# Casting two weight blocks ahead of the bank copies, and making the last block's sum sooner, in the seven-product groups of three feed-forwards

## The chip, the cores and the metric

The kernel runs on one core of a Trainium2 chip, as one program. The metric is the time of one execution on the device in microseconds; the median of several runs counts. Beside the runs there is one profiled execution, from which all rows below are taken.

## The reference, cut to what matters

A two-layer encoder trunk over 256 tokens of width 1024, all in float32. Each layer is a feed-forward, a token mixer (a convolution in the first layer, latent attention in the second), and another feed-forward. So there are four feed-forwards, and all four have the same shape:

```python
D_MODEL = 1024; SEQ = 256; D_FF = 2816

def swiglu_ffn(h, w1, w3, w2):
    return (jax.nn.silu(h @ w1) * (h @ w3)) @ w2

for i in range(DEPTH):
    h = h + FFN_RES_WEIGHT * swiglu_ffn(rmsnorm(h, ffn_norm1[i]), ffn1_w1[i], ffn1_w3[i], ffn1_w2[i])
    m = rmsnorm(h, mix_norm[i])
    ...  # h = h + conv_module(m, ...) or mla(m, ...)
    h = h + FFN_RES_WEIGHT * swiglu_ffn(rmsnorm(h, ffn_norm2[i]), ffn2_w1[i], ffn2_w3[i], ffn2_w2[i])
return rmsnorm(h, final_norm)
```

## The kernel before, in words

**Split numbers.** Each float32 operand is split into a high part (`hi`, rounded to the matmul's type) and a low part (`lo`, what the rounding left). A product of two operands is then three matmuls: low weights by high rows, high by high, high by low rows (`mm3`, lines 333, 336, 337). ScalarE casts the high part of a weight block (`hi<-raw`), VectorE subtracts it for the low part (`lo<-raw,hi`); each block is split in two pieces of 1024 columns, so there are two casts and two subtractions for each.

**Blocks.** Weights come as blocks of 128 x 2048 from memory, by SP's queue, into four `raw` buffers; `hi` and `lo` have five buffers each (`W_BUFS`). The list `blocks` holds them in the order of use. `load_to(n)` loads and splits blocks up to number n; `n_used` counts those in use.

**Seven products for eight.** In the up products of a feed-forward there are six chunks (c = 0 to 5) of 512 columns of `w1` and of `w3`. For chunk 3 (`SEVEN_UP`), and for the first part of the down products, the kernel replaces eight block products by seven, on sums and differences of blocks and of rows (`seven_products`). Such a group uses seven split blocks, here called block one to seven; in the code they are `n0` to `n0 + 6`, and `load_seven` makes them with j = 0 to 6. Blocks five and six are split from `raw` buffers that earlier subtractions left (j = 4 and 5). Block seven is split from one that has to be made first by a subtraction over the whole block, 128 x 2048 (`sub(b[11], b[21], b[11])`, called the sum of block seven). Block eight is the first block of chunk 4.

**The group's order.** Each of the seven products is 12 matmuls (four slices of rows, three each) into one of four accumulator banks, `c11`, `c21`, `c12`, `c22` in the code, `u` in the profile. Product one goes to c11; ScalarE then copies c11 to c21. Product two goes to c22; ScalarE copies c22 to SBUF (`kept`, in the profile `p`). Product three accumulates into c21; VectorE adds c21 and kept into c12 (the first addition of banks). Product four accumulates into c11, product five into c21, and VectorE adds c21 and kept into c22 (the second addition). Product six accumulates into c12, product seven into c21. So product five, which writes c21, has to wait for the first addition, which reads it. After the group ScalarE takes the activation of the first rows of tokens from c11 and of the second from c21, VectorE multiplies, and the result is turned (`gt` transpose, four transfers `gd`, one transfer `gb`) into the gates `Gh` and `Gl` for the down products.

**What sets the order.** The program is recorded in the order of the code and then scheduled once, at build time, by priorities and dependencies; each engine afterwards works through its own list in order. `urgent(...)` records an instruction with high priority, `order(a, b)` makes a come after b on the list. The lines that matter here: casts of a block are kept `behind` the last urgent instructions, and one low piece of block six and one of block seven come after the first and the second addition (`order(casts[n0 + 5, 0][1], add.ins)` and the same with 6).

Of the kernel before, what the change touches and what calls it, by code (L numbers as in the profile page):

```python
# [15 lines left out]
AF = mybir.ActivationFunctionType  # L16
# [26 lines left out]
PIECES = 2  # L43
# [46 lines left out]
def trunk(ctx: ExitStack, tc: tile.TileContext, x, xt, first, pos, invf, gfin, wdw,  # L90
          f1w13, f1w2, f2w13, f2w2, cw1, cw2, wa, wuq, wukv, wo, wpair, out):
    nc = tc.nc
# [12 lines left out]
    def uid(s):  # L105
        n_uid[0] += 1
        return f"{s}_{n_uid[0]}"
# [6 lines left out]

    def seven(four):

        group = {}
        return [("seven", j, four, group) for j in range(7)]  # L120

    blocks = []
    conv_block = {}
    for i in range(2):
        for w13, w2 in ((f1w13, f1w2), (f2w13, f2w2)):

            n_ffn = 2 * i + (w13 is f2w13)
            for cc_ in range(5):
                if cc_ in SEVEN_UP.get(n_ffn, ()):
                    four = [w13[i, m, 2 * cc_ + a_] for a_ in range(2) for m in range(2)]  # L130
                    blocks += seven(four)
                    continue
                for m in range(2):
                    blocks += [w13[i, m, 2 * cc_ + a_] for a_ in range(2)]
            blocks += [w13[i, a_, 10] for a_ in range(2)]
            if n_ffn in SEVEN_DOWN:
                blocks += seven([w2[i, a_] for a_ in range(4)])
            blocks += [w2[i, a_] for a_ in range(4 if n_ffn in SEVEN_DOWN else 0, NF // 2)]
            if w13 is f1w13:
                if i == 0:  # L140

                    for m in (-1, -2, -3, -4, *CONV_TILES):
                        blocks += [cw2[-m - 1] if m < 0 else ("whole", cw1[m])]
                        conv_block[m] = len(blocks) - 1
                else:
                    blocks += [wa[0], wa[1], wa[2][:, :1280], wa[3][:, :1280]]
                    blocks += [wuq[2], wuq[0], wukv[0], wukv[1], wuq[1]]
                    blocks += [wo[a_] for a_ in range(H // 2)]
    loaded = []
    n_used = [0]  # L150
# [3 lines left out]
    def order(ins, first):  # L154
        tc.add_manual_dep(ins.ins, first.name, mybir.DependencyInfo(
            mybir.DependencyClass.NoSync, mybir.DependencyReason.DATA), reason="order")

    def behind(ins):

        for first in ahead_of.get(ins.ins.engine, [])[-BEHIND:]:  # L160
            order(ins, first)


    casts = {}
# [18 lines left out]
    def fetched(src):  # L183
        raw = rawp.tile([P, HB], F32, tag="raw", name=uid("raw"))
        dma = nc.sync.dma_start(raw, src)
        if turns:
            order(dma, turns[-1].ins)
        return raw

    def load_seven(j, four, b, pieces):  # L190
        hi = wp.tile([P, HB], F32R, tag="hi", name=uid("hi"))
        lo = wp.tile([P, HB], F32R, tag="lo", name=uid("lo"))
        n = len(loaded)
        if j == 0:
            b[11], b[12] = fetched(four[0]), fetched(four[1])
        elif j == 1:
            b[22] = fetched(four[3])
        elif j == 2:
            b[21] = fetched(four[2])
        def sub(out, left, right):  # L200
            ins = nc.vector.tensor_sub(out, left, right)  # L201
            behind(ins)
            return ins

        if j == 1:
            sub(b[11], b[12], b[11])
            sub(b[12], b[22], b[12])
        elif j == 2:
            thirds[n] = sub(b[11], b[22], b[11])
        elif j == 6:  # L210
            sub(b[11], b[21], b[11])
        raw = b[(11, 11, 11, 21, 12, 22, 11)[j]]
        for i in range(pieces):
            c = slice(i * HB // pieces, (i + 1) * HB // pieces)
            casts[n, i] = nc.scalar.copy(hi[:, c], raw[:, c]), sub(lo[:, c], raw[:, c], hi[:, c].bitcast(F32))  # L215
            behind(casts[n, i][0])
        return hi, lo
# [35 lines left out]
    def urgent(f):  # L253

        def g(*args, **kw):
            traced = nc.cur_bb.bb.instructions
            n = len(traced)
            with tc.high_priority():
                r = f(*args, **kw)
            last = {ins.engine: ins for ins in traced[n:]}  # L260
            for engine, ins in last.items():
                ahead_of.setdefault(engine, []).append(ins)
            return r
        return g

    def load_ahead(ahead=W_BUFS - 2):
        load_to(min(len(blocks), n_used[0] + ahead))

    def load_to(last):
        while len(loaded) < last:  # L270
            loaded.append(load(blocks[len(loaded)], PIECES))
# [98 lines left out]
            out[n] = [z[:, i].rearrange("p (k t) -> p k t", t=P) for z in (sh, sl)]  # L370
        return out

    def seven_products(xh, xl, forms, banks, late={}):


        def rows(a, tb):
            k = slice(4 * a, 4 * a + 4)
            return xh[:, k, tbs(tb)], xl[:, k, tbs(tb)]

        def product(a, b, fresh):  # L380
            load_ahead(W_BUFS - 1)
            (hi, lo), = weights(1, False)
            for k in range(4):
                c = slice(k * 512, k * 512 + 512)
                before[:] = [mm3(b, a[0][:, k], a[1][:, k], hi[:, c], lo[:, c], fresh and k == 0, k == 3, before, True)]

        n0 = n_used[0]
        before = []
        c11, c21, c12, c22 = banks[0, 0], banks[1, 0], banks[0, 1], banks[1, 1]
        product(rows(0, 0), c11, True)  # L390
        first = urgent(nc.scalar.copy)(c21, c11)
        for cast in late.values():
            order(cast, first.ins)
        product(forms[0], c22, True)
        kept = tmp.tile([P, 512], F32, tag="s", name=uid("p5"))
        urgent(nc.scalar.copy)(kept, c22)
        product(forms[1], c21, False)
        add = urgent(nc.vector.tensor_add)(c12, c21, kept)
        order(casts[n0 + 5, 0][1], add.ins)
        for high, low in gates[-2 * NT:-NT] if not late else ():  # L400
            order(low, thirds[n0 + 2].ins)
        late_gates = []
        for high, low in gates[-NT:] if not late else ():
            late_gates.append((high, low))
        product(rows(1, 0), c11, False)
        product(forms[2], c21, False)
        add = urgent(nc.vector.tensor_add)(c22, c21, kept)
        order(casts[n0 + 6, 0][1], add.ins)
        for n, (high, low) in enumerate(late_gates):
            order(high, casts[n0 + 5 + n, PIECES - 1][0].ins)  # L410
            order(low, casts[n0 + 7, PIECES - 1][1].ins)
        product(forms[3], c12, False)
        product(rows(1, 1), c21, False)
# [8 lines left out]
    def tbs(tb):  # L422
        return slice(tb * P, (tb + 1) * P)
# [427 lines left out]
    def ffn_in(act, X, make_next, beside, apart, seven_up, seven_down):  # L851
# [48 lines left out]
        for c in range(6):  # L900

            both = c == 5
            w = 256 if both else 512
            kn = HB // 512
            u = {}
            if c == 0 and X.pool:
                first_chunk(X, u)
            if seven_up and c == min(seven_up) - 2:
                after = [casts[5, PIECES - 1][1]] if X.whole else ()
                forms = forms_of(sums_of_rows(*whole_rows(X.xh, X.xl, after)), Gh[:, 14:], Gl[:, 14:])  # L910
            if both and seven_down:
                down()
            if c in seven_up:
                for key in ((0, 0), (0, 1), (1, 1), (1, 0)):
                    u[key] = bank("A", "u")
                seven_products(X.xh, X.xl, forms, {(tb, m): b for (m, tb), b in u.items()})
                beside()
                beside()
            for m in range(0 if u else 1 if both else 2):
# [18 lines left out]
                for i, (k, tb, *kinds) in enumerate(steps):  # L938
                    hi, lo = parts[k // kn]
                    j = k % kn  # L940
# [26 lines left out]
                    beside()  # L967
            for tb in range(NT):
                s = tmp.tile([P, 512], F32, tag="s", name=uid("s"))
                nc.scalar.activation(s[:, :w], u[0, tb][:, :w], AF.Silu, scale=X.r[tb])  # L970
                mul = urgent(nc.vector.tensor_mul) if c in seven_up or c + 1 in seven_up else nc.vector.tensor_mul
                mul(s[:, :w], s[:, :w], u[0, tb][:, w:] if both else u[1, tb])
                turn(c, tb, w, s)
        o = Rows(Gh, Gl, NF, make_next is Final, seven_down)
        if seven_down:
            both = (xp.tile([P, KT, S], F32R, tag=tag, name=uid("rows")) for tag in ("Xh", "Xl"))
            late = {2: None, 3: None}
# [753 lines left out]
    class Rows512:  # L1731

        n = {"ht": 0, "hb": 0}
# [11 lines left out]
    def beside():  # L1745

        next(todo, None)

    X = Norm("ffn1_0", half=True)
    first_rows(X)  # L1750
    X.whole = True
    X = ffn(X, lambda act: Plain("mix_0", act), beside)
    for _ in todo:
        pass
    X = conv(X, lambda act: Norm("ffn2_0", half=True, turn_by_dma=rows))
    apart.close()
    X = ffn(X, lambda act: Norm("ffn1_1", half=True, turn_by_dma=rows), apart=True)
    X = ffn(X, lambda act: Norm("mix_1", turn_by_dma=rows), apart=True)
    cc, sn, _ = tables
    X = mla(X, lambda act: Norm("ffn2_1", half=True, turn_by_dma=rows), cc, sn)  # L1760
# [102 lines left out]
```

## Time and profile before

| | us |
|---|---|
| median of 3 runs | 892.23 |
| the runs | 892.22, 894.73, 892.23 |
| profiled execution | 891.44 |
| its span in the profile | 889.5 |
| TensorE busy | 882.0 (99%) |
| VectorE busy | 770.4 (87%) |
| ScalarE busy | 580.2 (65%) |
| TensorE's waits, in all | 1.4 |

The span is what lies between the first and the last instruction in the trace; 1.94 us of the profiled execution lie around it. In the rows PE is TensorE, DVE VectorE, ACT ScalarE, POOL GpSimd and SP the queue that issues transfers. L201 is line 201 of the kernel. A row of a timeline has the start in us from the span's start, the duration in us, the engine, line, operation and operands (written tile, then those read), and in brackets the idle time before it and what ended it. The three groups that the change touches are those of feed-forward two (its first matmul at 337.41 us), three (511.5 us) and four (774.4 us). Busy time of TensorE counts modelled ends of matmuls, so its short waits are better read from the starts of neighbouring matmuls.

### The profile page before, as it was taken

The numbers are of one execution on the slowest core, as the hardware profiler recorded it, in microseconds if no ns is written. First come the engines' busy times: TensorE is split into PE (matmuls) and PEld (weight loads), VectorE is DVE, ScalarE is ACT, GpSimd is POOL, SyncE is SP. The second block draws the span as 40 slices with busy tenths as digits, with TensorE's granted clock in tenths as the row PEclk, the third lists the DMA queues.
The fourth block names the chain that finished last, engine by engine and source line by source line (L and its number), as shares of the span: only waits on it lengthen the run. The fifth ranks groups of instructions, "written<-read, shape, count | busy, mean of one in ns | idle before, by whom it ended". The sixth has DMA issues, their size and how long they took to land.

```text
span 889.5 us, 12294 instructions
## 1 busy us (share of the span) xinstructions
PE 882.0 (99%) x4209; PEld 741.9 (83%) x4209; DVE 770.4 (87%) x1114; ACT 580.2 (65%) x1005; POOL 104.8 (12%) x227
## 2 busy tenths in 40 slices
PE   9999999999999999999999999999999999999997
PEld 7888887898988888888888888888899888888886
DVE  6899999789999998999498989995778689989973
ACT  7667868789887655657275465673676666474752
POOL 1000000079952000000010000001400010000000
PEclk9999999999999999999999999999999999999999
DMA  9884929834216855939759378495643549287541
GB/s 338 297 308 161 398 80 374 300 132 153 96 60 225 307 213 194 365 93 393 251 179 344 97 249 318 142 386 183 221 147 142 190 155 368 80 300 276 192 190 48
DMA packets 71054, 198.94 MB, mean 224 GB/s; under 512 B 12368, under 2 KB 41936, under 8 KB 51664
## 3 DMA queue, kind: packets, MB, share of 16 engines
q1 hardware_dynamic: 70560, 197.47, 61.9%
q8 instruction: 33, 0.54, 0.2%
q10 hardware_dynamic: 432, 0.69, 0.2%
q14 instruction: 29, 0.24, 0.1%
HBM read 181.87 MB, written 16.25 MB: 223 GB/s over the span
## 4 chain that ended last, share of the span: by engine, by line
PE 98%; DVE 1%; issue 0%; ACT 0%; ACTq 0%; DVEq 0%
PE u L333 17%; PE u L337 17%; PE u L336 17%; PE o L333 9%; PE o L337 9%; PE o L336 9%; PE u L1019 3%; PE gate L1019 3%; PE o L1255 3%; PE u L418 2%; PE sc L1616 1%; PE tp L453 1%; PE pairs L1062 1%; DVE lo L201 1%; PE a L337 1%; PE a L336 1%
## 5 line engine op out<-in xcount | busy, mean ns | idle before, releaser
L248 DVE TENSOR_TENSOR lo<-raw,hi 128x1024 fp32r<-128x1024 f32 (+1 forms) x228 | 266.8, 1210 | 29.2 <-ACT hi L247 28.5
L247 ACT CAST hi<-raw 128x1024 fp32r<-128x1024 f32 (+1 forms) x230 | 228.5, 1044 | 72.1 <-DMA raw<-in_f2w 24.3
L337 PE MATMUL u<-hi,Xl 128*128 128x512 f32 x592 | 230.4, 389 | 0.0
L336 PE MATMUL u<-hi,Xh 128*128 128x512 f32 x592 | 230.3, 389 | 0.0
L333 PE MATMUL u<-lo,Xh 128*128 128x512 f32 x592 | 230.2, 389 | 0.0
L215 ACT CAST hi<-raw 128x1024 fp32r<-128x1024 f32 x112 | 111.7, 1049 | 56.7 <-DVE raw L201 46.4
L201 DVE TENSOR_TENSOR lo<-raw,hi 128x1024 fp32r<-128x1024 f32 x112 | 132.0, 1215 | 6.6 <-ACT hi L215 6.5
L337 PEld LDWEIGHTS u<-hi,Xl 128*128 128x128 f32 x592 | 111.1, 188 | 23.6 <-DVE Xl L472 0.5
L336 PEld LDWEIGHTS u<-hi,Xh 128*128 128x128 f32 x592 | 111.1, 188 | 23.1
L333 PEld LDWEIGHTS u<-lo,Xh 128*128 128x128 f32 x592 | 111.1, 188 | 22.9
L333 PE MATMUL o<-lo,Gh 128*128 128x512 f32 (+1 forms) x276 | 106.7, 386 | 0.0
L336 PE MATMUL o<-hi,Gh 128*128 128x512 f32 (+1 forms) x276 | 106.5, 386 | 0.0
L337 PE MATMUL o<-hi,Gl 128*128 128x512 f32 (+1 forms) x276 | 106.5, 386 | 0.0
L444 POOL TENSOR_TENSOR ms<-ss 128x1 f32<-128x1 f32 x16 | 8.1, 509 | 592.8 <-ACT junk L436 592.8
L201 DVE TENSOR_TENSOR raw<-raw,raw 128x2048 f32<-128x2048 f32 x32 | 73.1, 2285 | 0.8 <-DMA raw<-in_f1w 0.2
L333 PEld LDWEIGHTS o<-lo,Gh 128*128 128x128 f32 x276 | 51.8, 188 | 10.6 <-DVE lo L201 0.2
L337 PEld LDWEIGHTS o<-hi,Gl 128*128 128x128 f32 x276 | 51.8, 188 | 10.5
L336 PEld LDWEIGHTS o<-hi,Gh 128*128 128x128 f32 x276 | 51.8, 188 | 10.4
L1108 DVE SCALAR_TENSOR_TENSOR acc<-V,dw,acc 128x128 f32<-128x128 f32 (+1 forms) x174 | 53.9, 390 | 0.0
L970 ACT ACTIVATE s<-u,R 128x512 f32<-128x512 f32 (+1 forms) x48 | 30.9, 647 | 29.5 <-PE u L337 28.7
L1129 ACT ACTIVATE prod<-V,dw 128x128 f32<-128x128 f32 (+1 forms) x128 | 45.6, 415 | 1.9 <-POOL Y L1130 1.0
L806 DVE SCALAR_TENSOR_TENSOR h<-o,rh,h 128x512 f32<-128x512 f32 (+1 forms) x18 | 12.9, 719 | 29.0 <-PE o L337 29.0
(269 smaller groups left out, 1306.6 us busy)
## 6 DMA issues: line engine op xcount, KB each, us to landing
raw<-in_f2w SPq DMA_DIRECT2D x66, 1024.0 KB, 5.6
raw<-in_f1w SPq DMA_DIRECT2D x62, 1024.0 KB, 6.9
raw<-in_cw SPq DMA_DIRECT2D x12, 1024.0 KB, 5.2
gd<-gt SPq DMA_DIRECT2D x160, 64.0 KB, 2.9
gb<-gd SPq DMA_DIRECT2D x24, 256.0 KB, 2.8
rows<-gd SPq DMA_DIRECT2D x16, 256.0 KB, 3.3
raw<-in_wo SPq DMA_DIRECT2D x4, 1024.0 KB, 4.7
hd<-rows SPq DMA_DIRECT2D x56, 64.0 KB, 2.3
```

The lines of the kernel that those rows point to most:

```text
L201: ins = nc.vector.tensor_sub(out, left, right)
L215: casts[n, i] = nc.scalar.copy(hi[:, c], raw[:, c]), sub(lo[:, c], raw[:, c], hi[:, c].bitcast(F32))
L247: casts[len(loaded), i] = (nc.scalar.copy(hi[:, c], raw[:, c]), low.tensor_sub(lo[:, c], raw[:, c], hi[:, c].bitcast(F32)))
L248: low.tensor_sub(lo[:, c], raw[:, c], hi[:, c].bitcast(F32)))
L333: mm = nc.tensor.matmul(o, ah, bl, start=start, stop=False, skip_group_check=seeded)
L336: nc.tensor.matmul(o, ah, bh, start=False, stop=False, skip_group_check=seeded)
L337: return nc.tensor.matmul(o, al, bh, start=False, stop=stop, skip_group_check=seeded)
L970: nc.scalar.activation(s[:, :w], u[0, tb][:, :w], AF.Silu, scale=X.r[tb])
L1019: mm = nc.tensor.matmul(u[:, t], w[:, c], X.x[:, k, t], start=(k == 0), stop=(k == KT - 1))
L1108: dve_last.append(nc.vector.scalar_tensor_tensor(out if j == j1 - 1 else y, v, w, y, op0=ALU.mult, op1=ALU.add))
L1129: prods_last.append(nc.scalar.activation(p, v, AF.Copy, scale=w))
L1255: p = nc.tensor.matmul(o[tb, d], (Zl if kind == "x" else Zh)[:, f, tbs(tb)], (lo if kind == "l" else hi)[:, c], start=(f, kind) == (0, "l" ...
```

## The change

Three things, in the up products' group of feed-forwards two, three and four (`ahead`, and `last` 5; feed-forward one keeps its order):

- ScalarE's casts of block five come ahead of the first bank copy, and those of block six ahead of the second.
- The sum of block seven is made when block six is loaded (j = 5) and not when block seven is (j = 6), so it may stand earlier in VectorE's list. For that the low pieces which come after the two additions are those of block seven and block eight, both pieces, and no longer one piece of block six and of block seven.
- In the last chunk (of all four feed-forwards) the casts of a later block come after the first activation.

```diff
-    def seven(four):
-        group = {}
+    def seven(four, last):
+        group = {"last": last}
         return [("seven", j, four, group) for j in range(7)]
...
-                    blocks += seven(four)
+                    blocks += seven(four, 5 if n_ffn else 6)
...
-                blocks += seven([w2[i, a_] for a_ in range(4)])
+                blocks += seven([w2[i, a_] for a_ in range(4)], 6)
...
-        elif j == 6:
+        elif j == b["last"]:
             sub(b[11], b[21], b[11])
...
-    def seven_products(xh, xl, forms, banks, late={}):
+    def seven_products(xh, xl, forms, banks, late={}, ahead=False):
...
+        def copy(to, b, block):
+            if not ahead:
+                return urgent(nc.scalar.copy)(to, b)
+            load_to(block + 1)
+            ins = urgent(nc.scalar.copy)(to, b)
+            order(ins, casts[block, PIECES - 1][0].ins)
+            return ins
         product(rows(0, 0), c11, True)
-        first = urgent(nc.scalar.copy)(c21, c11)
+        first = copy(c21, c11, n0 + 4)
...
-        urgent(nc.scalar.copy)(kept, c22)
+        copy(kept, c22, n0 + 5)
         product(forms[1], c21, False)
         add = urgent(nc.vector.tensor_add)(c12, c21, kept)
-        order(casts[n0 + 5, 0][1], add.ins)
+        if ahead:
+            load_to(n0 + 7)
+        for i in range(PIECES if ahead else 1):
+            order(casts[n0 + (6 if ahead else 5), i][1], add.ins)
...
         add = urgent(nc.vector.tensor_add)(c22, c21, kept)
-        order(casts[n0 + 6, 0][1], add.ins)
+        if ahead:
+            load_to(n0 + 8)
+        for i in range(PIECES if ahead else 1):
+            order(casts[n0 + (7 if ahead else 6), i][1], add.ins)
         for n, (high, low) in enumerate(late_gates):
-            order(high, casts[n0 + 5 + n, PIECES - 1][0].ins)
+            order(high, casts[n0 + (6 if ahead else 5) + n, PIECES - 1][0].ins)
...
-                seven_products(X.xh, X.xl, forms, {(tb, m): b for (m, tb), b in u.items()})
+                seven_products(X.xh, X.xl, forms, {(tb, m): b for (m, tb), b in u.items()}, ahead=not X.whole)
...
-                nc.scalar.activation(s[:, :w], u[0, tb][:, :w], AF.Silu, scale=X.r[tb])
+                silu = nc.scalar.activation(s[:, :w], u[0, tb][:, :w], AF.Silu, scale=X.r[tb])
+                if both and seven_down and tb == 0:
+                    load_to(n_used[0] + 3)
+                    for i in range(PIECES):
+                        order(casts[n_used[0] + 2, i][0], silu.ins)
```

VectorE in the group of feed-forward two, before. lo_558 are the low pieces of block four, lo_560 of block five, lo_563 of block six, lo_565 of block seven, lo_568 of block eight; u_556<-u_554 is the first addition (c12 from c21), u_555<-u_554 the second (c22 from c21), raw_533<-raw_542 the sum of block seven, gt_550 a transpose of chunk 2:

```order
L201 TENSOR_TENSOR lo_558_3462<-raw_542_3372,hi_557_3461 128x1024 x2
L485 STREAM_TRANSPOSE gt_550_3446<-s_549_3443 128x512
L201 TENSOR_TENSOR lo_560_3481<-raw_534_3304,hi_559_3480 128x1024 x2
L201 TENSOR_TENSOR lo_563_3501<-raw_539_3362,hi_562_3500 128x1024
L259 TENSOR_TENSOR u_556_3460<-u_554_3458,p5_561_3498 128x512
L201 TENSOR_TENSOR lo_563_3501<-raw_539_3362,hi_562_3500 128x1024
L201 TENSOR_TENSOR raw_533_3302<-raw_542_3372,raw_533_3302 128x2048
L259 TENSOR_TENSOR u_555_3459<-u_554_3458,p5_561_3498 128x512
L201 TENSOR_TENSOR lo_565_3520<-raw_533_3302,hi_564_3519 128x1024 x2
```

The same place now:

```order
L202 TENSOR_TENSOR lo_558_3462<-raw_542_3372,hi_557_3461 128x1024 x2
L202 TENSOR_TENSOR raw_533_3302<-raw_542_3372,raw_533_3302 128x2048
L202 TENSOR_TENSOR lo_560_3480<-raw_534_3304,hi_559_3479 128x1024
L501 STREAM_TRANSPOSE gt_550_3446<-s_549_3443 128x512
L202 TENSOR_TENSOR lo_560_3480<-raw_534_3304,hi_559_3479 128x1024
L202 TENSOR_TENSOR lo_563_3500<-raw_539_3362,hi_562_3499 128x1024 x2
L260 TENSOR_TENSOR u_556_3460<-u_554_3458,p5_561_3498 128x512
L202 TENSOR_TENSOR lo_565_3521<-raw_533_3302,hi_564_3520 128x1024 x2
L260 TENSOR_TENSOR u_555_3459<-u_554_3458,p5_561_3498 128x512
L249 TENSOR_TENSOR lo_568_3540<-raw_566_3538,hi_567_3539 128x1024 x2
```

The sum of block seven has moved from behind the first addition to the place right after block four's low pieces; both low pieces of block six stand ahead of the first addition, and both of block seven ahead of the second.

ScalarE in the same group, before. hi_559 are the casts of block five, hi_562 of block six, hi_564 of block seven, hi_567 of block eight; u_554<-u_553 is the first bank copy, p5_561<-u_555 the second, s_575<-u_553 the activation of c11:

```order
L259 COPY u_554_3458<-u_553_3457 128x512
L215 CAST hi_559_3480<-raw_534_3304 128x1024 x2
L259 COPY p5_561_3498<-u_555_3459 128x512
L215 CAST hi_562_3500<-raw_539_3362 128x1024 x2
L862 CAST Gh_470_2920<-gb_548_3439 128x4x128
L970 ACTIVATE s_575_3599<-u_553_3457,R_465_2859 128x512
L215 CAST hi_564_3519<-raw_533_3302 128x1024 x2
L862 CAST Gh_470_2920<-gb_552_3453 128x4x128
L247 CAST hi_567_3539<-raw_566_3538 128x1024 x2
```

And now:

```order
L216 CAST hi_559_3479<-raw_534_3304 128x1024 x2
L260 COPY u_554_3458<-u_553_3457 128x512
L216 CAST hi_562_3499<-raw_539_3362 128x1024 x2
L260 COPY p5_561_3498<-u_555_3459 128x512
L216 CAST hi_564_3520<-raw_533_3302 128x1024 x2
L878 CAST Gh_470_2920<-gb_548_3439 128x4x128
L248 CAST hi_567_3539<-raw_566_3538 128x1024 x2
L986 ACTIVATE s_575_3599<-u_553_3457,R_465_2859 128x512
```

Each pair of casts has moved up by one copy, and the casts of block eight stand ahead of the activation. In the groups of feed-forwards three and four the rows move in the same way. On SP's queue the load of block eight (raw_566) now stands ahead of the four transfers of a turn (gd_551), and three later loads ahead of the next turn's. On TensorE only chunk 4 changes: all 24 matmuls of the first rows of tokens now come before those of the second, where they took turns every six matmuls.

## The prediction

> **What bounds the kernel now.** I read the page first, then the waits of the tensor engine, the busy time by stretches, and the timelines of single engines in the three places that the change touches. Busy times, and the chain that ended last:
>
> ```profile
> PE 882.0 (99%) x4209; PEld 741.9 (83%) x4209; DVE 770.4 (87%) x1114; ACT 580.2 (65%) x1005; POOL 104.8 (12%) x227
> ...
> PE 98%; DVE 1%; issue 0%; ACT 0%; ACTq 0%; DVEq 0%
> ```
>
> TensorE carries 98% of the chain. But ends of matmuls are modelled here (0.39 us each), so a short wait can hide under "busy". The honest reading is from start to start. The list of TensorE's waits has one after the warm-up, in feed-forward one (total, times, longest, in us):
>
> ```profile
> PE o L333 <- DVE lo L201: 0.4, 1, 0.4
> ```
>
> The busy time of a stretch inside feed-forward three, its columns named in the first line:
>
> ```profile
> core 0: us, PE busy (x) PEld busy (x) DVE busy (x) ACT busy (x) POOL busy (x), PEclk, DMA share, GB/s
> 445.00:575.00 130.00, 130.00 (x576) 107.63 (x575) 120.83 (x135) 79.59 (x107) 3.21 (x4) 1.00 0.62 217
> ```
>
> And TensorE's timeline at that one wait (start, duration, engine, line, operation, operands):
>
> ```profile
> 135.96 0.39 PE L337 MATMUL o<-hi,rows 128*128 128x512 f32 x1
> 136.75 0.47 PE L333 MATMUL o<-lo,rows 128*128 128x512 f32 x1 [0.40 <-DVE lo L201]
> 137.05 0.40 PE L336 MATMUL o<-hi,rows 128*128 128x512 f32 x1
> 137.29 0.39 PE L337 MATMUL o<-hi,rows 128*128 128x512 f32 x1
> ```
>
> 576 matmuls lie in 130 us or reach into it, some two of them from before: one every 0.227 us, with the clock granted in full. A pause shows as in the last rows: 0.79 us between two starts instead of 0.227, so 0.56 lost, though the list of waits counts only 0.40; the next start comes 0.30 later, another 0.07 lost. Now the four starts that matter: the first product of the group in feed-forward two, and the fifth product of each of the three groups.
>
> ```profile
> 337.41 0.39 PE L333 MATMUL u<-lo,Xh 128*128 128x512 f32 x1
> ...
> 348.29 0.39 PE L333 MATMUL u<-lo,Gh 128*128 128x512 f32 x1
> ...
> 522.37 0.39 PE L333 MATMUL u<-lo,Gh 128*128 128x512 f32 x1
> ...
> 785.27 0.39 PE L333 MATMUL u<-lo,Gh 128*128 128x512 f32 x1
> ```
>
> From 337.41 to 348.29 are four products of 12 matmuls: 10.88 / 48 = 0.2267. So TensorE loses nothing there: **the group has no stall that a better order could remove.** The most that the change can win in this execution is nothing; what it can do is make a wait. So the question is whose slack it uses.
>
> **The change part by part.** VectorE's timeline in the group of feed-forward two, with idle time and its releaser in brackets:
>
> ```profile
> 338.38 2.35 DVE L201 TENSOR_TENSOR lo<-raw,hi 128x1024 fp32r<-128x1024 f32 x2
> 340.65 0.70 DVE L485 STREAM_TRANSPOSE gt<-s 128x512 f32<-128x512 f32 x1
> 341.95 2.36 DVE L201 TENSOR_TENSOR lo<-raw,hi 128x1024 fp32r<-128x1024 f32 x2 [0.60 <-ACT hi L215]
> 345.57 1.22 DVE L201 TENSOR_TENSOR lo<-raw,hi 128x1024 fp32r<-128x1024 f32 x1 [1.25 <-ACT hi L215]
> 346.71 0.69 DVE L259 TENSOR_TENSOR u<-u,p 128x512 f32<-128x512 f32 x1
> 347.31 1.22 DVE L201 TENSOR_TENSOR lo<-raw,hi 128x1024 fp32r<-128x1024 f32 x1
> 348.44 2.29 DVE L201 TENSOR_TENSOR raw<-raw,raw 128x2048 f32<-128x2048 f32 x1
> 351.21 0.70 DVE L259 TENSOR_TENSOR u<-u,p 128x512 f32<-128x512 f32 x1 [0.49 <-PE u L337]
> 351.84 2.36 DVE L201 TENSOR_TENSOR lo<-raw,hi 128x1024 fp32r<-128x1024 f32 x2
> ...
> 354.72 1.22 DVE L248 TENSOR_TENSOR lo<-raw,hi 128x1024 fp32r<-128x1024 f32 x1
> ```
>
> In order: low parts of block four, a transpose, low parts of block five, half of block six, the first addition of banks (346.71), the other half, the sum of block seven (348.44), the second addition, block seven's low parts, then the next chunk. ScalarE beside it:
>
> ```profile
> 340.39 0.57 ACT L259 COPY u<-u 128x512 f32<-128x512 f32 x1 [5.64 <-PE u L337]
> 340.87 2.00 ACT L215 CAST hi<-raw 128x1024 fp32r<-128x1024 f32 x2
> 343.05 0.59 ACT L259 COPY p<-u 128x512 f32<-128x512 f32 x1 [0.18 <-PE u L337]
> 343.54 2.00 ACT L215 CAST hi<-raw 128x1024 fp32r<-128x1024 f32 x2
> ...
> 348.49 0.69 ACT L970 ACTIVATE s<-u,R 128x512 f32<-128x512 f32 x1 [2.44 <-PE u L337]
> 350.76 2.01 ACT L215 CAST hi<-raw 128x1024 fp32r<-128x1024 f32 x2 [1.58 <-DVE raw L201]
> ```
>
> *Casts ahead of the copies (ScalarE): 0.* ScalarE idles 5.64 us before the first copy. Block five's casts fit there: their buffers are free when the first product starts (337.41), 2.00 us later they are done (339.4), and the copy still starts at 340.39. Block six's casts take the place that block five's had (340.87 to 342.87), ahead of the second copy at 343.05: 0.18 us of cover is left. If it went, the copy would be late by as much, and its reader, the first addition, comes 4 us later. Free.
>
> *Block seven's sum made sooner, and all of block six ahead of the first addition (VectorE): the cost.* In VectorE's queue the addition now stands behind the sum, a transpose and four low halves (blocks five and six). It starts no sooner than these are through. Spacing in a full queue: lows 1.135 (338.38 to 340.65 for two), addition 0.60 (346.71 to 347.31), and for the sum and the transpose these two pairs of neighbours elsewhere:
>
> ```profile
> 133.18 2.28 DVE L201 TENSOR_TENSOR raw<-raw,raw 128x2048 f32<-128x2048 f32 x1
> 135.38 2.35 DVE L201 TENSOR_TENSOR lo<-raw,hi 128x1024 fp32r<-128x1024 f32 x2
> ...
> 355.85 0.70 DVE L485 STREAM_TRANSPOSE gt<-s 128x512 f32<-128x512 f32 x1
> 356.48 1.18 DVE L248 TENSOR_TENSOR lo<-raw,hi 128x1024 fp32r<-128x1024 f32 x1
> ```
>
> Sum 2.20, transpose 0.63. Together 2.20 + 4 x 1.135 + 0.63 = 7.37 us after the lows of block four. These end their turn at 340.65, so the addition starts at 348.02 and ends at 348.71. Two idle stretches (0.60 and 1.25) lay ahead of it; the early casts let VectorE fill them, but sum and half block are 3.3 us of new work there.
>
> Who waits: the fifth product accumulates into the bank (c21) that this addition reads, and starts at 348.29. Before, the addition was over at 347.40, 0.89 us early. Now it ends 0.42 us late. TensorE takes its matmuls in order, so everything behind waits too, with no idle time to give it back. What waking costs is in the pause quoted above: VectorE's first half of the pair at 135.38 ended about 1.22 later (136.60), TensorE started at 136.75: 0.15. And 0.1 for the slower starts after it (0.07 and what follows). So 0.42 + 0.15 + 0.1 = 0.67 us in feed-forward two.
>
> The other two groups (in feed-forward three the lows of block four, then the transpose whose place the sum takes; in four the transpose alone):
>
> ```profile
> 512.30 2.35 DVE L201 TENSOR_TENSOR lo<-raw,hi 128x1024 fp32r<-128x1024 f32 x2
> 514.57 0.70 DVE L485 STREAM_TRANSPOSE gt<-s 128x512 f32<-128x512 f32 x1
> ...
> 777.47 0.70 DVE L485 STREAM_TRANSPOSE gt<-s 128x512 f32<-128x512 f32 x1
> ```
>
> 514.57 + 7.37 + 0.69 = 522.63 against 522.37: 0.26 late; 777.47 + 8.06 = 785.53 against 785.27: 0.26 late. With 0.25 each for waking: 0.51 and 0.51. **Sum: 0.67 + 0.51 + 0.51 = 1.7 us.** From below: waking at 0.03 (the sum ended at 350.73, ScalarE's cast followed at 350.76) and no slow starts, 0.45 + 0.29 + 0.29 = 1.0. From above: the addition held once more in each group by as long as VectorE idled for ScalarE at 341.35, 0.6, makes 3.5. I take 1.7: its waking is TensorE's own.
>
> *What comes sooner: worth 0.* Block seven's first low half ended at about 353.0 (half of the pair at 351.84); the seventh product wants it at 348.29 + 24 x 0.2267 = 353.73: 0.7 spare. Block eight's first half ended at 355.94 and is wanted at 356.45: 0.5 spare. Both come 2 to 3 us sooner after the change. Spare time that grows shortens nothing. The second addition still follows the fifth product; VectorE is through with block seven by 351.0, before that product ends.
>
> *TensorE's order in the next chunk: 0.* It does all 24 matmuls of the first rows of tokens before the second's, so block nine is wanted 2.7 us sooner, at 356.45 + 0.67 + 12 x 0.2267 = 359.8. VectorE, from the second addition at 351.7: 0.60, two lows, one gate (0.6), one low half: through at 356.3.
>
> *SP's queue: 0.* Block eight's load goes ahead of a turn's four transfers, and three later loads go ahead of the next turn's; the gates that these bring are read by the down products, over 30 us later. ScalarE's casts of block eight now stand ahead of the activation of the group's first bank (348.49 before), so it waits for this load. Issues with median time to landing, and the range of all loads:
>
> ```profile
> raw<-in_f2w SPq DMA_DIRECT2D x66, 1024.0 KB, 5.6
> ...
> DMA to landing us min/median/max: 3.4/6.0/12.5
> ```
>
> Issued when the sum is through (342.9), landed at 348.5, casts to 350.5, activation to 351.2; its bank is wanted at 356.45. The remaining moves (a low half against a sum in the down products, gates later) swap work of equal length.
>
> **The sum against the clock.** The profiled execution took 891.44 us (span 889.5 and 1.94 around). 891.44 + 1.7 = 893.1. The median of the runs, 892.23, is 0.8 above it; on that footing 893.9, which I give. About 0.3% (2.7 us) is what a measurement of this kernel can tell from no change; 1.7 is 0.2%.
>
> **Rivals.** That the change does nothing is not one: the order shown with it has sum and low halves ahead of the addition.
> 1. *Slower: ScalarE's queue is held by the load.* A landing after 354.4 (356.45 and the 0.67 of the pause, less casts 2.0 and activation 0.69) delays the next chunk's first product one for one: that decides at 11.5 us from issue. For: the longest load took 12.5. Against: the median of 5.6. At 12.5 in all three groups 3 x 1.0 + 1.7 = 4.7, so 896.9. Chance 0.05.
> 2. *Slower: the addition is later than worked out,* by one more wait for ScalarE, the upper bound above: 3.5, so 895.7. Against: block six's casts end at 342.87, three microseconds before VectorE wants them. Chance 0.09.
> 3. *Nothing shows: the thin spots pay back.* The runs' median lies 0.8 above the profiled one; if that is lost where 0.5 and 0.7 us are spare, the change removes it: 1.7 - 0.8 = 0.9, so 893.1. For: those are the smallest margins of the three stages. Against: the profiled execution shows no such loss. Chance 0.14.
> 4. *Faster: the pace itself is a wait.* The shortest steady spacing of long matmuls in the trace is the convolution's (another form, 256 columns; 16 to a row):
>
> ```profile
> 210.31 3.62 PE L1019 MATMUL gate<-Xp,raw 128*128 128x256 f32 x16
> 213.76 3.62 PE L1019 MATMUL u<-Xp,raw 128*128 128x256 f32 x16
> ```
>
> 3.45 / 16 = 0.216. If the 0.011 us above it were waiting for casts, the 84 matmuls of each group could win 252 x 0.011 = 2.8, and with no late addition 889.4. Against: ScalarE idled through the whole first product (5.64 us up to 340.39), and the group kept the 0.2267 of the long stretch. Chance 0.02. The Trainium skill, "TensorE: Matmul & The Clock Gate", section "Wait — 56ns, not 53.3ns?", gives 215.7 ns for back-to-back matmuls of 512 columns at full clock, where this case's rows have 226.7; by it the sum would be -2.8 + 1.7, or 891.1. No row here shows that difference to be a wait.
>
> **How the numbers follow.** The forecast (1.0 to 2.7 us more) has 0.70: 893.9. With rival 3 most of the chance lies within 0.3%; rivals 1 and 2 and a scatter of the runs (892.22 to 894.73 already) give slower 0.14; rival 4 and what I overlook give faster 0.03; the same 0.83. The range leaves out the long loads and the fast pace: from 892.0 (no cost, and the scatter) to 895.5 (just under the upper bound).
>
> **What would show it.** Right: between the last matmul of product four and the first of product five 0.6 to 0.9 us instead of 0.227, three times, with VectorE's u<-u,p as the releaser, and nowhere else a new pause; u<-u,p starting at about 348.0; block seven's lows done before 351.1. Wrong: no pause there (then VectorE was through sooner, or TensorE does not wait for that addition); pauses at the next chunk's start with a load or the activation ahead of them (rival 1); a pace other than 0.227.

## The result and the profile after

| | before | after |
|---|---|---|
| median of 20 runs, us | 892.23 | 894.34 |
| range of the runs, us | 891.38 to 894.73 | 893.24 to 895.88 |
| span of the profiled execution, us | 889.5 | 892.4 |

The ratio is 1.0021, 95% interval 1.0015 to 1.0028: slower by 1.9 us (1.3 to 2.5); the two medians lie 2.1 apart. The forecast was 1.7 us slower, 893.9 us, in a range from 892.0 to 895.5.

The page after, busy times and the chain that ended last (share of the span by engine):

```profile
PE 883.5 (99%) x4209; PEld 742.5 (83%) x4209; DVE 769.7 (86%) x1114; ACT 581.4 (65%) x1005; POOL 105.0 (12%) x227
...
PE 74%; DVE 14%; DMA 7%; issue 3%; SPq 1%; ACT 1%; DVEq 0%; ACTq 0%
```

The chain ran along TensorE for 98% of the span, now for 74%: where TensorE waits, the chain leaves it and follows VectorE back to what made VectorE late. 14% of the chain on VectorE does not mean that 14% of the time was lost there. How much was lost stands between the starts of matmuls. TensorE's timeline at the change from product four (`Xl` last) to product five (`Gh` first), in the three groups:

```profile
348.53 0.39 PE L338 MATMUL u<-hi,Xl 128*128 128x512 f32 x1
349.42 0.50 PE L334 MATMUL u<-lo,Gh 128*128 128x512 f32 x1 [0.50 <-DVE u L260]
349.76 0.40 PE L337 MATMUL u<-hi,Gh 128*128 128x512 f32 x1
...
523.44 0.39 PE L338 MATMUL u<-hi,Xl 128*128 128x512 f32 x1
523.95 0.50 PE L334 MATMUL u<-lo,Gh 128*128 128x512 f32 x1
...
786.80 0.39 PE L338 MATMUL u<-hi,Xl 128*128 128x512 f32 x1
788.04 0.50 PE L334 MATMUL u<-lo,Gh 128*128 128x512 f32 x1 [0.85 <-DVE u L260]
```

Each time one start of 0.227 us has become 0.89, 0.51 and 1.24, and the next one 0.34 (349.42 to 349.76, and the same in the other two). Lost: 0.66 + 0.11, 0.28 + 0.11, 1.01 + 0.11, together 2.3 us. The span grew by 2.9; 0.46 of that was there before the first group began (its first matmul at 337.88 instead of 337.41). The list of TensorE's waits shows less, since it measures from modelled ends of matmuls:

```profile
PE u L334 <- DVE u L260: 1.3, 2, 0.9
```

Two pauses of three, 1.3 us of 2.3. The Trainium skill, "Perfetto Trace Analysis", section "Tensor Engine Instruction (MATMUL, LD_WEIGHTS)", says that the end of a matmul in a profile is computed and not observed; these rows agree: a matmul is shown for 0.39 us although the next one starts 0.227 us later.

VectorE's timeline in the group of feed-forward two:

```profile
341.33 2.28 DVE L202 TENSOR_TENSOR raw<-raw,raw 128x2048 f32<-128x2048 f32 x1
343.53 1.22 DVE L202 TENSOR_TENSOR lo<-raw,hi 128x1024 fp32r<-128x1024 f32 x1
344.67 0.70 DVE L501 STREAM_TRANSPOSE gt<-s 128x512 f32<-128x512 f32 x1
345.30 3.46 DVE L202 TENSOR_TENSOR lo<-raw,hi 128x1024 fp32r<-128x1024 f32 x3
348.67 0.69 DVE L260 TENSOR_TENSOR u<-u,p 128x512 f32<-128x512 f32 x1
349.27 2.35 DVE L202 TENSOR_TENSOR lo<-raw,hi 128x1024 fp32r<-128x1024 f32 x2
352.51 0.70 DVE L260 TENSOR_TENSOR u<-u,p 128x512 f32<-128x512 f32 x1 [0.89 <-PE u L338]
```

No idle time stands between the sum (341.33) and the first addition (348.67): 7.34 us of work. The addition ends at 349.36 and product five starts at 349.42. Behind it nothing is short: block seven's lows are through at 351.6, and the second addition has time to wait 0.89 us for TensorE. ScalarE beside it:

```profile
338.13 2.00 ACT L216 CAST hi<-raw 128x1024 fp32r<-128x1024 f32 x2 [2.81 <-PE u L338]
340.85 0.57 ACT L260 COPY u<-u 128x512 f32<-128x512 f32 x1 [0.72 <-PE u L338]
341.33 2.00 ACT L216 CAST hi<-raw 128x1024 fp32r<-128x1024 f32 x2
343.52 0.59 ACT L260 COPY p<-u 128x512 f32<-128x512 f32 x1 [0.18 <-PE u L338]
...
348.79 2.00 ACT L248 CAST hi<-raw 128x1024 fp32r<-128x1024 f32 x2 [2.27 <-DMA raw<-in_f2w]
350.69 0.68 ACT L986 ACTIVATE s<-u,R 128x512 f32<-128x512 f32 x1
```

The early casts cost nothing: both copies still wait for TensorE, the second with the 0.18 us of cover that it had. Block eight's casts do hold ScalarE for their load (2.27 us), but the activation behind them comes at 350.69, some 6 us before its bank is wanted.

### The profile page after: what moved, and what is told of

Same layout as the page of the kernel before. It is cut to its first block, busy times and chain, and to the rows that moved or that the text cites. A ratio compares the mean times of both kernels' runs of the same rounds, so it can differ in the third digit from the quotient of the medians.

```text
span 892.4 us, 12294 instructions
## 1 busy us (share of the span) xinstructions
PE 883.5 (99%) x4209; PEld 742.5 (83%) x4209; DVE 769.7 (86%) x1114; ACT 581.4 (65%) x1005; POOL 105.0 (12%) x227
## 4 chain that ended last, share of the span: by engine, by line
PE 74%; DVE 14%; DMA 7%; issue 3%; SPq 1%; ACT 1%; DVEq 0%; ACTq 0%
PE u L334 9%; PE u L338 9%; PE u L337 9%; PE o L334 9%; PE o L338 9%; PE o L337 9%; DVE lo L202 4%; PE u L1039 3%; PE gate L1039 3%; PE u L434 2%; DVE lo L249 2%; DVE raw L202 2%; DMA raw<-in_f2w 2%; DMA gd<-gt 2%; DVE gt L501 1%
```

## The experiments

The theory: all of the loss is product five waiting for the first addition of banks, which two things delay in VectorE's list, the sum of block seven (2.20 us) and one more low half of block six (1.135 us). The rival: the moved casts, loads and the order elsewhere cost the time. Four kernels first.

**half_after** puts one low half back behind the addition and keeps the rest:

```diff
-        for i in range(PIECES if ahead else 1):
-            order(casts[n0 + (6 if ahead else 5), i][1], add.ins)
+        order(casts[n0 + 5, PIECES - 1 if ahead else 0][1], add.ins)
+        for i in range(PIECES if ahead else 0):
+            order(casts[n0 + 6, i][1], add.ins)
```

> The changed kernel with one thing put back: one low half of block six (1.135 us of VectorE) again stands after the first addition of banks, in all three groups. The sum of block seven stays early, and so do all moved casts and loads. Theory (product five waits for the first addition, which stands behind the sum and four low halves): the addition now comes 2.20 + 3 x 1.135 + 0.63 = 6.2 us after the lows of block four instead of 7.3, which is before product five is due in all three groups (in the third, where VectorE came 0.7 us later in the profile, by 0.2 us only). No pause ahead of product five, three starts of matmuls 0.227 us apart, and the time of the kernel before: 0 +- 0.5 us against it. Rival (the moved casts, loads or the order on TensorE cost the time, and the pause is only where it shows): still +1.9 us against the kernel before, with new pauses elsewhere.

Measured: ratio to the kernel before 0.9996 (0.9988 to 1.0005). VectorE and TensorE in the group of feed-forward two:

```profile
341.98 2.29 DVE L202 TENSOR_TENSOR raw<-raw,raw 128x2048 f32<-128x2048 f32 x1
...
345.95 2.32 DVE L202 TENSOR_TENSOR lo<-raw,hi 128x1024 fp32r<-128x1024 f32 x2
348.18 0.70 DVE L260 TENSOR_TENSOR u<-u,p 128x512 f32<-128x512 f32 x1
```

```profile
349.40 0.39 PE L338 MATMUL u<-hi,Xl 128*128 128x512 f32 x1
349.63 0.39 PE L334 MATMUL u<-lo,Gh 128*128 128x512 f32 x1
```

From the sum to the addition are 6.20 us instead of 7.34; the addition is over at 348.88, 0.75 before product five, and the pause is gone here and in the other two groups. All moved casts and loads are still there, so they cost nothing that these runs can tell.

**sum_back** takes the other delay away (`seven(four, 6)` for all feed-forwards, so that the sum is made after the addition; nothing else).

> The changed kernel with the other delay put back: the sum of block seven (2.20 us of VectorE) is made when block seven is loaded, after the first addition; all four low halves of blocks five and six stay ahead of it, and all casts and loads stay moved. Theory: the addition comes when product three has left its bank or 4 x 1.135 + 0.63 = 5.2 us after the lows of block four, whichever is later, 1 us or more before product five; no pause, the time of the kernel before: 0 +- 0.5 us. Rival (the casts, loads and TensorE's order cost the time): +1.9 us.

Measured: 0.9995 (0.9986 to 1.0004). VectorE and TensorE in feed-forward two:

```profile
346.46 0.70 DVE L260 TENSOR_TENSOR u<-u,p 128x512 f32<-128x512 f32 x1
347.07 2.28 DVE L202 TENSOR_TENSOR raw<-raw,raw 128x2048 f32<-128x2048 f32 x1
```

```profile
348.92 0.39 PE L334 MATMUL u<-lo,Gh 128*128 128x512 f32 x1
```

The addition was over at 347.16, 1.75 us before product five, with the sum behind it. Each of the two delays alone fits into the slack; both together do not.

**low_twice** adds to the delay:

```diff
+            if j == b["last"] == 5 and i == pieces - 1:
+                again[n] = sub(lo[:, c], raw[:, c], hi[:, c].bitcast(F32))
...
+            order(add, again[n0 + 5].ins)
```

> The changed kernel with more of the suspected delay: one low half of block six is computed twice ahead of the first addition (1.135 us more of VectorE in each of the three groups). Theory: each microsecond ahead of the addition now goes straight to TensorE; three pauses longer by 1.135 us each: +3.4 us against the changed kernel, +5.3 us against the kernel before. Rival (the pause is set by something else, and VectorE has time to spare there): no more than the changed kernel, +1.9 us; a partial gain between the two would mean that some of the extra work falls into idle time of VectorE.

Measured: 1.0078 (1.0058 to 1.0097), slower by 7.0 us (5.2 to 8.7). TensorE at product five, three times:

```profile
349.30 0.39 PE L341 MATMUL u<-hi,Xl 128*128 128x512 f32 x1
351.22 0.50 PE L337 MATMUL u<-lo,Gh 128*128 128x512 f32 x1 [1.53 <-DVE u L263]
...
525.21 0.39 PE L341 MATMUL u<-hi,Xl 128*128 128x512 f32 x1
527.07 0.50 PE L337 MATMUL u<-lo,Gh 128*128 128x512 f32 x1 [1.48 <-DVE u L263]
...
789.91 0.39 PE L341 MATMUL u<-hi,Xl 128*128 128x512 f32 x1
791.68 0.50 PE L337 MATMUL u<-lo,Gh 128*128 128x512 f32 x1 [1.38 <-DVE u L263]
```

Pauses of 1.92, 1.86 and 1.77 us from start to start, 5.2 us lost with the slow second starts: extra work ahead of the addition goes straight to TensorE. The runs' ratio lies 1.8 us above that, and the trace shows no other new pause in the three groups. The six executions differ in their granted clock: the three with 0.998 or more took 897.48 to 898.41 us, 5.2 to 6.1 above the median of the kernel before (892.29); the three with 0.994 to 0.996 took 900.29 to 902.85. So the excess goes with a lower clock in half of the runs. Why it was lower is not shown.

**silu_back** drops the last chunk's part (`if False:` in place of `if both and seven_down and tb == 0:`).

> The changed kernel without its part in the last chunk (the casts of a later block after the first activation). Everything in the three groups stays as changed. Theory: that part costs nothing, so the time is that of the changed kernel: +1.9 us (1.4 to 2.4) against the kernel before, with three pauses ahead of product five. Rival (that part costs a share of the loss, for example by making VectorE late on its way into the third group, where the pause in the profile was 1.1 us and 0.5 was worked out): +1.3 us or less against the kernel before, and a pause of about 0.5 us in the third group.

Measured: 1.0061 (1.0047 to 1.0074), slower by 5.4 us (4.2 to 6.6); both expectations missed. The pauses at product five were there (0.67, 0.51, 0.97 us from start to start), and a new one in the down products of feed-forward two. TensorE, then ScalarE ahead of it:

```profile
393.08 0.39 PE L338 MATMUL o<-hi,Gl 128*128 128x512 f32 x1
395.03 0.50 PE L334 MATMUL o<-lo,s1h 128*128 128x512 f32 x1 [1.56 <-DVE s L992]
```

```profile
388.92 3.91 ACT L216 CAST hi<-raw 128x1024 fp32r<-128x1024 f32 x4 [6.33 <-DVE raw L202]
392.73 0.47 ACT L986 ACTIVATE s<-u,R 128x256 f32<-128x256 f32 x1
```

Four casts, which waited 6.33 us for a sum on VectorE, now stand ahead of the last chunk's first activation (392.73), and VectorE's product with it (`s`, L992) is late for the down products. With the part, the activation is ahead of these casts (387.87 against 388.24 in the changed kernel), and so it is in the kernel before. So another part of the change pushes these casts ahead, and the part that looked idle puts the activation back in front. Which one was not tried alone; it is not the early sum by itself, since sum_only, below, has no such part and the activation still comes first. A second new pause (1.05 us from 449.34 on, ahead of the first matmul of feed-forward three) waited for a transfer of rows; as the changed kernel's second profile has one at the same place (0.51 from start to start), it is not put down to the part. In this profile 1.8 us are lost at product five, 2.1 in the down products and 1.4 at the start of feed-forward three.

Three more runs followed.

**half_silu_back** joins half_after and silu_back.

> Two things put back into the changed kernel: one low half of block six stands after the first addition again, as in half_after, and the last chunk's part is left out, as in silu_back. The sum and the casts of the group stay early. The order on ScalarE then has four casts of the down products, which wait for a sum on VectorE, ahead of the last chunk's first activation, in feed-forwards two, three and four; with the part, and in the kernel before, the activation is ahead. Theory (two costs that add): no pause before product five, but the pauses that silu_back showed in the down products, 1.8 us in feed-forward two and 0.3 in three, and, if its late start of feed-forward three (1.3 us, behind a transfer of rows) follows from them, that too: +2.1 to +3.6 us against the kernel before. Rival (silu_back's extra time came only together with the late addition, or from its run): 0 +- 0.5 us.

Measured: 1.0032 (1.0019 to 1.0044), slower by 2.9 us (1.7 to 3.9). Product five comes without a pause in all three groups, and the down products wait for the same `s`, this time in feed-forwards three and four, not in two and three as expected:

```profile
566.58 0.39 PE L338 MATMUL o<-hi,Gl 128*128 128x512 f32 x1
567.38 0.50 PE L334 MATMUL o<-lo,s1h 128*128 128x512 f32 x1 [0.41 <-DVE s L993]
...
830.23 0.39 PE L338 MATMUL o<-hi,Gl 128*128 128x512 f32 x1
831.56 0.50 PE L334 MATMUL o<-lo,s1h 128*128 128x512 f32 x1 [0.94 <-DVE s L993]
```

With the slow second starts this profile loses 1.9 us at the two places, inside the interval of the runs. Within the intervals the two costs add up: 2.9 here and 1.9 of the change make 4.8, and silu_back has 4.2 to 6.6.

**sum_only** makes only the sum sooner in the kernel before (`last` 5, no `ahead`, no last chunk's part).

> The kernel before with one part of the change alone: the sum of block seven is made with block six, so it stands ahead of the first addition on VectorE; the casts keep their places behind the bank copies, one half of block six stays after the addition, and the last chunk has no added order (the activation is ahead of the casts there anyway). Theory: in the third place of VectorE's list the sum fills the two waits for ScalarE (0.60 and 1.25 us) and 0.35 us more; the addition comes 2.20 + 3 x 1.135 + 0.63 = 6.2 us after block four's lows, as it does in the kernel before with its waits, and before product five is due. No pause, 0 +- 0.5 us against the kernel before. Rival (the early sum by itself delays what the tensor engine waits for): +1 us or more, with the pauses before product five.

Measured: 1.0025 (1.0014 to 1.0037), slower by 2.2 us; the theory missed, and the rival's place was wrong too. In feed-forward two the addition was just in time, in three early, in four 0.18 us late: 0.5 us in the groups. The rest is in the down products. The profiled execution was the slowest of nine (897.66 of 892.39 to 897.66), so its 4 us there are an upper end. TensorE in feed-forward two, and VectorE ahead of it:

```profile
396.13 0.50 PE L333 MATMUL o<-lo,rows 128*128 128x512 f32 x1 [0.16 <-ACT o L259]
396.47 0.40 PE L336 MATMUL o<-hi,rows 128*128 128x512 f32 x1
397.18 0.50 PE L337 MATMUL o<-hi,rows 128*128 128x512 f32 x1 [0.31 <-DVE rows L369]
```

```profile
376.03 0.69 DVE L862 TENSOR_TENSOR Gl<-gb,Gh 128x512 fp32r<-128x512 f32 x1 [1.33 <-ACT Gh L862]
376.64 2.29 DVE L201 TENSOR_TENSOR raw<-raw,raw 128x2048 f32<-128x2048 f32 x1
...
381.56 2.29 DVE L201 TENSOR_TENSOR raw<-raw,raw 128x2048 f32<-128x2048 f32 x1 [2.04 <-DMA raw<-in_f2w]
```

A gate (`Gl<-gb,Gh`) has moved directly ahead of the first sum of the down products and waits 1.33 us there; the second sum then waits 2.04 for its load. The changed kernel has the same two waits (1.54 and 1.52 us) and no pause there, so they alone do not explain it. What differs is when that load is issued: at 373.92 here, after three transfers of a turn (372.39 to 373.33) on SP's queue, against 370.93 in the changed kernel and 370.32 in the kernel before. That VectorE reaches the down products late is shown, and the late load is one step on the way; which of the moved instructions is to blame was not tried.

**after_look** is the changed kernel once more, for its profile alone, because the third pause (1.24) had been more than twice the second.

> The changed kernel as it is, once more, for its profile. In the first profile VectorE began block four's lows in the third group 1.55 us after the first matmul of product one, in the second 0.80, and the pauses were 1.24 and 0.51 us from start to start. Theory (that lateness belongs to one execution: a transfer that landed late before the group): a third group that begins at about 0.8 us, with a pause of 0.5, as in low_twice, where it began at 0.80. Rival (it belongs to the changed order): 1.3 to 1.6 us again and a pause of 1.0 or more.

Measured: 894.84 us, and 0.65, 0.51 and 0.51 us from start to start. VectorE at block four's lows and at the addition, and TensorE at product one and at product five, in the third group:

```profile
778.19 2.35 DVE L202 TENSOR_TENSOR lo<-raw,hi 128x1024 fp32r<-128x1024 f32 x2
...
787.80 0.69 DVE L260 TENSOR_TENSOR u<-u,p 128x512 f32<-128x512 f32 x1
```

```profile
777.39 0.39 PE L334 MATMUL u<-lo,Xh 128*128 128x512 f32 x1
...
788.04 0.39 PE L338 MATMUL u<-hi,Xl 128*128 128x512 f32 x1
788.54 0.50 PE L334 MATMUL u<-lo,Gh 128*128 128x512 f32 x1
```

Block four's lows begin 0.80 us after product one; in the first profile of the same kernel it was 1.55:

```profile
776.14 0.39 PE L334 MATMUL u<-lo,Xh 128*128 128x512 f32 x1
```

```profile
777.69 2.34 DVE L202 TENSOR_TENSOR lo<-raw,hi 128x1024 fp32r<-128x1024 f32 x2
```

So the long third pause belonged to one execution. All profiles together show how it works. "Entry" is the start of block four's lows after the first matmul of product one; the last column is how late the first addition ended against the start at which product five was due (negative: early), all from the timelines:

| kernel, group | entry, us | low halves ahead of the addition, beside the sum | addition late by, us |
|---|---|---|---|
| half_after, 3 | 0.80 | 3 | -0.91 |
| half_after, 2 | 0.97 | 3 | -0.75 |
| half_silu_back, 4 | 1.14 | 3 | -0.59 |
| sum_only, 2 | 1.68 | 3 | -0.04 |
| sum_only, 4 | 1.91 | 3 | +0.18 |
| after_look, 3 and 4 | 0.80 | 4 | +0.22 |
| after_look, 2 | 0.96 | 4 | +0.37 |
| after, 2 | 1.18 | 4 | +0.60 |
| after, 4 | 1.55 | 4 | +0.96 |

(Groups by feed-forward; those of the changed kernel, silu_back, half_after, half_silu_back and sum_only that are not listed follow the same two lines.) Within 0.02, the last column is the entry less 1.71 with three lows, and less 0.58 with four; the difference of the two constants is one low half, 1.13 us. With four the addition is late even at the earliest entry seen (0.80), so TensorE waits in every one of these groups, and a later entry is passed on in full. With three it can be 0.9 us later before TensorE feels it.

No version here beats the kernel before; half_after and sum_back equal it, since TensorE has no wait in these groups to lose.

## Why the prediction was right, step by step

- *TensorE has no stall in the groups to remove:* right, as far as the runs can tell. half_after and sum_back have the sooner blocks seven and eight too, and stay at 0.9996 and 0.9995. The pace of 0.227 was kept everywhere; rival 4 gained nothing.
- *Casts ahead of the copies cost 0:* right, with the 0.18 us of cover still there.
- *7.37 us from block four's lows to the addition:* 7.34 in the trace. The addition at "about 348.0" came at 348.67, of which 0.46 is the later start of the whole group and 0.2 a later entry.
- *The three terms, 0.67 + 0.51 + 0.51 = 1.7:* after_look, with entries near those of the profile before, has 0.54 + 0.39 + 0.39 = 1.3; the first profile, with two late entries, 0.77 + 0.39 + 1.12 = 2.3. The runs say 1.9. Within the terms the lateness was nearly right (0.42, 0.26 and 0.26; in after_look 0.37, 0.22 and 0.22), and the waking was mis-sized: 0.15 was worked out from half of a pair of lows, and the addition's own row gives 0.06 (349.36 to 349.42). The slow second start was right (0.1; 0.11). What the sum lacked is the scatter of the entry. The kernel before absorbs it in VectorE's two waits for casts (0.60 and 1.25 us): at entries of 0.97, 0.80 and 0.80 its addition ended 0.89 us early all three times. The changed order has no such wait left ahead of the addition. The two errors nearly cancelled, so that 1.7 came this close to 1.9 is in part luck.
- *The sign, 0.6 to 0.9 us three times and nowhere else a new pause:* the place and what TensorE waits for were right, the sizes only in part: 0.89, 0.51 and 1.24 in the first profile, 0.65, 0.51 and 0.51 in the second. The second also lost 0.9 us at the start of feed-forward three, behind a transfer of rows; whether the change brings that about was not tested.
- *The upper bound, 3.5, came from a wait for ScalarE:* no such wait was seen. The late entries are a scatter of that size from another source. In the first profile VectorE had waited for a gate's cast 24 us before the third group and had not caught up; the cast had waited for a transfer:

```profile
751.19 0.62 ACT L878 CAST Gh<-rows 128x512 fp32r<-128x512 f32 x1 [1.48 <-DMA rows<-gd]
751.84 0.69 DVE L878 TENSOR_TENSOR Gl<-rows,Gh 128x512 fp32r<-128x512 f32 x1 [1.19 <-ACT Gh L878]
```

  In the kernel before, VectorE waited 0.39 us at this place. All nine profiles fit together here. Where this gate starts on VectorE 25.2 to 25.9 us before the group's first matmul (before, half_after, low_twice, after_look), VectorE catches up with TensorE and the entry is 0.80 us. Where it starts 24.71, 24.58, 24.30, 24.20 and 23.94 us before (half_silu_back, silu_back, after, sum_back, sum_only), the entry is 1.14, 1.28, 1.55, 1.65 and 1.91: the two add up to 25.85 us each time, within 0.01. On the way VectorE idles in none of these five, but for the same 0.26 us right behind the gate. So a transfer that lands late is passed on in full to the entry, some 26 us later. Why it landed later in some executions is not shown.
- *Rival 1, a load in front of the activation:* the casts waited for it as worked out (landed at 348.8, forecast 348.5), and the activation had some 6 us to spare.
- *Rival 3, thin spots pay back:* half_after widens the same margins and shows no gain. Its interval, from 1.1 us faster to 0.4 slower, would still hold the 0.8 us, but the profile of the kernel before has no loss at these places.
- *Remaining moves "swap work of equal length", 0:* right for the whole change, but for a weaker reason than the text had. Taken apart, the last chunk's part was worth about 3 us against the order that the rest of the change brings about, and the early sum alone disturbed the down products.

## What to carry to other kernels

When a queue on a helper engine has slack ahead of an instruction that the bound engine waits for, count all that is moved ahead of it against that slack together, and leave room for the engine's scatter at the entry: here VectorE's idle time and slack took either of the two delays, not both, and with both in place a transfer that landed late reached TensorE. In a kernel whose order is scheduled as a whole, a part of a change that seems to do nothing may be what holds the rest in place; read the new order downstream before pricing a part at zero or undoing it. And read pauses of TensorE from start to start, since the list of waits held only 1.3 of 2.3 us.

## What the runs showed of the hardware

- TensorE started 0.05 to 0.06 us after VectorE's releasing instruction ended (349.36 to 349.42; in the third group 787.98 to 788.04). After each pause the first matmul is shown with 0.50 us and the next start follows 0.34 us later instead of 0.227, at every pause at product five: 0.11 us more for each pause, whatever its length (0.24 and 0.46 from start to start in sum_only, up to 1.92 in low_twice).
- VectorE's low halves last 1.22 us and follow each other every 1.13 us when they are independent: the next starts about 0.09 before the end of the one ahead. The repeat in low_twice, which writes the output of the one ahead once more, came 1.26 us after it, 0.04 past its end. The Trainium skill, "VectorE: DVE Perf Modes", section "The DRAIN you can't avoid", says that the next instruction does not start until the pipeline is empty, and that one that is not "held" starts earlier. The independent neighbours here start before the end that the profile shows, and the dependent one after it; whether that end is when the pipeline is empty, no run here shows.
